# S5 inputs moved into the merge, moments made in the chain, down projection's first groups in passes

## The chip, the cores and the metric

The kernel runs on one core of a Trainium2 chip. The metric is the device time of one execution in microseconds (us), the median of several runs. TensorE (PE in the profile) multiplies matrices; VectorE (DVE), ScalarE (ACT), GpSimd (POOL) and SyncE (SP) do the rest and issue the DMAs. Each engine works through its own list of instructions in order, and an instruction that waits for another engine holds up all that stand behind it on its own.

## The reference, cut to what matters

One layer of a decoder with a hybrid token mixer, in float32, with T = 1024 tokens and 1024 channels:

```python
h = rms_norm(x, norm_mix_pre)
proj = h @ w_in          # RWKV columns | S5 input u | two gates
gates = jax.nn.sigmoid(proj[..., N_RWKV_COLS + S5_WIDTH:] + b_gate)
g_rwkv, g_s5 = jnp.split(gates, 2, axis=-1)
o_rwkv = rwkv7_branch(p_rwkv, ...) @ w_branch_rwkv
o_s5 = s5_branch(u_s5, ...) @ w_branch_s5
mixed = (g_rwkv * o_rwkv + g_s5 * o_s5) @ w_out
x = x + rms_norm(mixed, norm_mix_post)
h = rms_norm(x, norm_ffn_pre)
f = conv_ffn(h, w_up, conv_w, conv_b, w_down)    # 1024 -> 2 x 2816 -> 1024
x = x + rms_norm(f, norm_ffn_post)
```

In the RWKV branch a state S of 64 x 64 per head is carried over the tokens, and each head's outputs y are normalised over their 64 channels; these sums over a head are the moments of this text:

```python
S = S * w_t + sa * b_t + v_t * k_t ; y_t = S r_t
mean = jnp.mean(y, axis=-1, keepdims=True)
var = jnp.mean(jnp.square(y - mean), axis=-1, keepdims=True)
y = ((y - mean) * lax.rsqrt(var + LNX_EPS)) * lnx_w + lnx_b
```

The S5 branch ends in `y = gelu(y)` and `y * sigmoid(y @ w_glu + b_glu)`; the gelu of its scan's result is what this text calls an S5 input (of the gated unit).

## The kernel before, in words

Channels lie on the 128 partitions, time on the free axis, in two halves of 512 tokens. Each operand of a large product is split into a high part (a cast on ACT, lines 160 and 245) and a low part (a subtraction on DVE, lines 161 and 246), and each product is three matmuls of 128 x 128 by 128 x 512: high by high, high by low, low by high (lines 180, 181 and 182; in the down projection 1760, 1761 and 1762).

The stages, by the span's time: norm and input projection with the S5 scan (to 255 us); RWKV, gates and merge (to 760); output projection, norms and up projection (to 1290); down projection (to 1517); last norm.

RWKV is made in four units: two groups of four heads by two time halves, unit i having group i % 2 and half i // 2. Each unit runs through a front (operands `ar` and `bk`, masked products `gr` at lines 752 and 754, line 741 making the last part of `bk`), an inverse of small triangular matrices on DVE (lines 810 and 812, fed by the masked products through DMAs of POOL at lines 760 and 803), a level step (lines 835 to 841: transposes on DVE, products on PE, copies on ACT), a chain of eight chunks (lines 850 to 913) in which each chunk's state S (line 912) is read by the next chunk's matmuls (line 887), and an end, `rwkv_out`, which normalises the chunk outputs `yn` and transposes them (line 961).

The order of the instructions on PE is written out by hand: a planner interleaves the lanes of the units with a queue of fill work (gate tiles, gated sums, merged sums) by due times, the constants named T_. On the other engines a scheduler puts the instructions in order beforehand, by priority and dependence. So a step that one function issues can stand, on DVE, ACT or POOL, among those of quite other functions.

Half 0's branches are merged while units 2 and 3 run. `merge_values` makes the merge's operands; it is called among the gate tiles, which fall into the front of unit 3. It loads the four S5 inputs of half 0 (`s5_y`: a DMA of POOL at line 1233 and a gelu on ACT at 1234) and splits them (`s5_split`: a strided cast at 1241 and a subtraction at 1242). `merge` then makes eight gated sums (`gate`, with the product at line 1264), from the fourth on with one tile of the gated unit each (`glu_tile`), which reads the S5 inputs; and then eight merged sums (lines 1264, 1269 and the split at 251).

The down projection is seven products by Winograd's form of Strassen's scheme, each over eleven slices of the inner dimension in six groups, (0,1), (2,3), (10), (4,5), (6,7), (8,9). A product accumulates into four PSUM banks m; a step is the three matmuls of one slice and one bank. Its operands are made a group ahead into a ring of three sets, from weights and activations that DMAs bring into stage tiles; line 1715 makes the sums and differences of them, line 1712 takes the banks out.

## Time and profile before

| | |
|---|---|
| runs shown | 1533.64, 1539.38, 1544.39 us; median 1539.38 |
| profiled execution | 1531.82 us, span 1530.0 |
| PE busy | 1473.2 us (96%) |
| DVE busy | 1152.2 us (75%) |
| ACT busy | 724.5 us (47%) |
| POOL busy | 181.4 us (12%) |
| mean granted PE clock | 0.991 |

Times in the trace count from the span's start. In a group's row, `rp<-ar,bk` names the output and the inputs of an instruction; a wait is told as the engine, the tile and the line that waited, and what it waited for. The granted clock is the share of full speed at which PE was let run in that stretch. [...]

### The profile page before, as it was taken

The numbers are of one execution on the slowest core, as the hardware profiler recorded it, in microseconds if no ns is written. First come the engines' busy times: TensorE is split into PE (matmuls) and PEld (weight loads), VectorE is DVE, ScalarE is ACT, GpSimd is POOL, SyncE is SP. The second block draws the span as 40 slices with busy tenths as digits, with TensorE's granted clock in tenths as the row PEclk, the third lists the DMA queues.
The fourth block names the chain that finished last, engine by engine and source line by source line (L and its number), as shares of the span: only waits on it lengthen the run. The fifth ranks groups of instructions, "written<-read, shape, count | busy, mean of one in ns | idle before, by whom it ended". The sixth has DMA issues, their size and how long they took to land.

```text
span 1530.0 us, 23482 instructions
## 1 busy us (share of the span) xinstructions
PE 1473.2 (96%) x8622; PEld 1175.9 (77%) x8622; DVE 1152.2 (75%) x2115; ACT 724.5 (47%) x1201; POOL 181.4 (12%) x340
## 2 busy tenths in 40 slices
PE   7999999999999989989999999999999999999997
PEld 5788787787677666666778788888888888788885
DVE  8879974765555594874668779788888887698777
ACT  6455444331454552556525556455555555443452
POOL 0022111124121223020110011000000000000000
PEclk9999999999999999999999999999999999999999
DMA  6355344444333446442455575333333336953722
GB/s 215 114 157 164 104 138 144 142 135 142 110 119 109 123 138 173 147 156 71 141 183 183 179 251 186 104 114 109 114 117 110 111 117 207 337 173 124 238 79 110
DMA packets 121556, 225.23 MB, mean 147 GB/s; under 512 B 31024, under 2 KB 37168, under 8 KB 121440
## 3 DMA queue, kind: packets, MB, share of 16 engines
q1 hardware_dynamic: 90576, 154.77, 31.7%
q0 software_dynamic: 21024, 64.71, 12.6%
q10 hardware_dynamic: 9840, 4.24, 1.0%
q8 instruction: 68, 1.11, 0.3%
q14 instruction: 48, 0.39, 0.1%
HBM read 164.16 MB, written 57.41 MB: 145 GB/s over the span
## 4 chain that ended last, share of the span: by engine, by line
PE 70%; DVE 15%; DMA 5%; issue 5%; ACT 4%; POOL 0%; SPq 0%; DVEq 0%; ACTq 0%; POOLq 0%
PE gm L180 9%; PE gm L181 7%; PE gm L182 7%; PE rp L1583 5%; PE rp L1584 5%; PE rp L1585 5%; PE mm L1584 2%; PE mm L1583 2%; PE mm L1585 2%; DMA st<-in_w_down_dram 2%; PE ch L181 2%; PE ch L182 2%; PE mm L180 2%; PE ch L180 2%; PE mm L181 2%
## 5 line engine op out<-in xcount | busy, mean ns | idle before, releaser
L180 PE MATMUL gm<-hh,wh 128*128 128x512 f32 x688 | 289.6, 421 | 3.0 <-DVE ev L1046 1.9
L181 PE MATMUL gm<-hl,wh 128*128 128x512 f32 x688 | 271.1, 394 | 1.6 <-DVE hl L246 1.6
L182 PE MATMUL gm<-hh,wl 128*128 128x512 f32 x688 | 270.8, 394 | 0.0
L160 ACT CAST wh<-wf 128x512 fp32r<-128x512 f32 x181 | 111.5, 619 | 169.8 <-PE gm L181 92.9
L161 DVE TENSOR_TENSOR wl<-wf,wh 128x512 fp32r<-128x512 f32 x181 | 124.0, 689 | 78.1 <-ACT wh L160 77.2
L180 PEld LDWEIGHTS gm<-hh,wh 128*128 128x128 f32 x688 | 130.1, 189 | 36.3 <-DVE ev L1046 2.3
L182 PEld LDWEIGHTS gm<-hh,wl 128*128 128x128 f32 x688 | 130.0, 189 | 28.5
L181 PEld LDWEIGHTS gm<-hl,wh 128*128 128x128 f32 x688 | 130.4, 190 | 25.5 <-DVE hl L246 3.6
L1761 PE MATMUL d<-xl,wh 128*128 128x512 f32 x308 | 120.3, 390 | 3.1 <-DVE xl L246 3.0
L1760 PE MATMUL d<-xh,wh 128*128 128x512 f32 x308 | 120.1, 390 | 0.0
L1762 PE MATMUL d<-xh,wl 128*128 128x512 f32 x308 | 119.9, 389 | 0.0
L1583 PE MATMUL rp<-t,h 128*128 128x512 f32 x252 | 98.3, 390 | 1.4 <-ACT p L1597 1.4
L1585 PE MATMUL rp<-t,l 128*128 128x512 f32 x252 | 98.0, 389 | 0.0
L1584 PE MATMUL rp<-t,h 128*128 128x512 f32 x252 | 98.0, 389 | 0.0
L1761 PEld LDWEIGHTS d<-xl,wh 128*128 128x128 f32 x308 | 57.8, 188 | 16.6 <-DVE xl L246 4.7
L246 DVE TENSOR_TENSOR l<-r,h 128x1024 fp32r<-128x1024 f32 (+1 forms) x40 | 38.9, 972 | 38.2 <-ACT h L245 38.2
L245 ACT CAST h<-r 128x1024 fp32r<-128x1024 f32 (+1 forms) x40 | 34.0, 849 | 70.1 <-PE rp L1584 65.9
L1760 PEld LDWEIGHTS d<-xh,wh 128*128 128x128 f32 x308 | 57.8, 188 | 12.0
L1762 PEld LDWEIGHTS d<-xh,wl 128*128 128x128 f32 x308 | 57.8, 188 | 11.8
L1604 DVE SCALAR_TENSOR_TENSOR y<-zv,vecs,y 128x1023 f32<-128x1023 f32 (+1 forms) x42 | 53.8, 1281 | 10.2 <-ACT y L1602 10.2
L1583 PEld LDWEIGHTS rp<-t,h 128*128 128x128 f32 x252 | 47.2, 187 | 12.0 <-ACT p L1597 2.2
L1584 PEld LDWEIGHTS rp<-t,h 128*128 128x128 f32 x252 | 47.3, 188 | 9.7
(472 smaller groups left out, 3324.7 us busy)
## 6 DMA issues: line engine op xcount, KB each, us to landing
r<-in_w_up_dram SPq DMA_DIRECT2D x42, 512.0 KB, 3.5
wf<-in_w_in_dram SPq DMA_DIRECT2D x72, 256.0 KB, 3.1
st<-in_w_down_dram SPq DMA_DIRECT2D x55, 256.0 KB, 4.2
st<-ACT SPq DMA_DIRECT2D x44, 256.0 KB, 4.7
ACT<-y POOLq DMA_DIRECT2D x21, 512.0 KB, 2.9
GT<-ev POOLq DMA_DIRECT2D x32, 256.0 KB, 3.4
wf<-in_w_br_dram SPq DMA_DIRECT2D x32, 256.0 KB, 3.1
wf<-in_w_out_dram SPq DMA_DIRECT2D x32, 256.0 KB, 2.7
```

The lines of the kernel that those rows point to most:

```text
L160: self.last_wh = nc.scalar.copy(h[:, :n], f[:, :n])
L161: low = nc.vector.tensor_tensor(l[:, :n], f[:, :n], h[:, :n].bitcast(F32), ALU.subtract)
L180: mm(ps, a, xh[k], start=a0, stop=False)
L181: mm(ps, a, xl[k], start=False, stop=False)
L182: mm(ps, b, xh[k], start=False, stop=z0)
L1583: mm(ps, wh[:, c], xh, start=first and k == 0, stop=False, skip_group_check=True)
L1584: mm(ps, wh[:, c], xl, start=False, stop=False, skip_group_check=True)
L1585: mm(ps, wl[:, c], xh, start=False, stop=k == 3, skip_group_check=True)
L1604: V.scalar_tensor_tensor(y[:, lag:], z[:, 0:1024 - lag], self.vec(nme, i), y[:, lag:], ALU.mult, ALU.add)
L1760: mm(ps, wh[:, c], xh[:, x], start=start, stop=False, skip_group_check=True)
L1761: mm(ps, wh[:, c], xl[:, x], start=False, stop=False, skip_group_check=True)
L1762: mm(ps, wl[:, c], xh[:, x], start=False, stop=stop, skip_group_check=True)
```

## The change

Three parts, and constants.

1. **S5 inputs.** `merge_values` no longer loads, gelus and splits half 0's four S5 inputs. `merge` does it at gated sums 1 and 2, two at each (table `XS0`), in tiles of the pool `ev` with its three buffers. On POOL their loads now stand singly among the stores of unit 3's masked products (line 760): two stores, load 0, a gate tile's store, load 1, two stores, load 2, the store of line 765, load 3, four stores.
2. **Moments.** The chain makes a quarter's moments after chunks 1, 3, 5 and 7: a reduction of 256 elements a partition on DVE, a subtraction of the mean on DVE, a square on ACT, a reduction on DVE. `rwkv_out` keeps the scale of the variance, the reciprocal root and the multiplication, this now in two halves, one for each pair u of heads.
3. **Down projection.** A step's matmuls are ordered (wh, xh), (wl, xh), (wh, xl). The first group of each product goes over its steps in three passes, one for each of these pairs, over all four banks (span 4: products 1, 2 and 3) or two banks at a time (span 2: the other four).

`T_LN` is not used where it falls (`rwkv_out`'s first yield is thrown away for units 0 to 2); `T_LF` puts the last unit's transposes four steps of three matmuls earlier among their neighbours on PE. Otherwise the order on PE is the same up to the down projection.

```diff
...
         mm = nc.tensor.matmul
         S, pt, UV, gr, ar, bkn = self.S[d["g"]], d["pt"], d["UV"], d["gr"], d["ar"], d["bkn"]
         d["yn"] = self.tg("yn", 1, (128, 4, 2, 2, 64))
+        d["lm"], d["lv"] = [self.small.tile([128, 16], F32, tag=n, name=self.nm(n), bufs=2) for n in ("lm", "lv")]
         kw = dict(stop=True, skip_group_check=True)
         uh = [(u, h, HS[h], HS[1 - h]) for u in range(2) for h in range(2)]
         t0, t1 = HS
...
                 mm(psn[sl, u], bkn[:, u, c, sl], UV[:, (c + h) % 8, h, u], start=False, **kw)
             for u in range(2):
                 V.scalar_tensor_tensor(S[:, u], psn[:, u], pt[:, c, u:u + 1], spt[:, u], ALU.mult, ALU.add)
+            if c % 2:
+                self.moments(d, c // 2)
             yield 0.65, T_CH
+
+    def moments(self, d, j):
+
+        V = self.nc.vector
+        y = d["yn"][:, j].rearrange("p u h i -> p (u h) i")
+        mean, var = d["lm"][:, 4 * j:4 * j + 4], d["lv"][:, 4 * j:4 * j + 4]
+        sq = d["ar"][:, 0, 2 * j:2 * j + 2].rearrange("p c t -> p (c t)").rearrange("p (a i) -> p a i", i=64)
+        V.tensor_reduce(mean, y, AX.X, ALU.add)
+        V.scalar_tensor_tensor(y, mean.unsqueeze(2).to_broadcast([128, 4, 64]), -1.0 / 64, y, ALU.mult, ALU.add)
+        self.nc.scalar.activation(sq, y, AF.Square)
+        V.tensor_reduce(var, sq, AX.X, ALU.add)

     def urgent(self, gen):

...
             return r
         if final:
             ts = [factors(u) for u in range(2)]
-        yn = d["yn"].rearrange("p c u h i -> p (c u h) i")
-        mean = self.small.tile([128, 16], F32, tag="lm", name=self.nm("lm"), bufs=2)
-        V.tensor_reduce(mean, yn, AX.X, ALU.add)
-        V.tensor_scalar(mean, mean, 1.0 / 64, None, ALU.mult)
-        V.tensor_tensor(yn, yn, mean.unsqueeze(2).to_broadcast([128, 16, 64]), ALU.subtract)
-        var = self.small.tile([128, 16], F32, tag="lv", name=self.nm("lv"), bufs=2)
-        for j in range(2):
-            sq = free[:, j].rearrange("p (a i) -> p a i", i=64)
-            A.activation(sq, yn[:, 8 * j:8 * j + 8], AF.Square)
-            V.tensor_reduce(var[:, 8 * j:8 * j + 8], sq, AX.X, ALU.add)
+        var = d["lv"]
         V.tensor_scalar(var, var, 1.0 / 64, 64e-5, ALU.mult, ALU.add)
-        y = self.rsqrt(var, 16, "or")
-        V.tensor_tensor(yn, yn, y.unsqueeze(2).to_broadcast([128, 16, 64]), ALU.mult)
+        y = self.rsqrt(var, 16, "or").rearrange("p (c u h) -> p c u h", u=2, h=2)
+        for u in range(2):
+            yn = d["yn"][:, :, u]
+            V.tensor_tensor(yn, yn, y[:, :, u].unsqueeze(3).to_broadcast([128, 4, 2, 64]), ALU.mult)
         if not final:
             ts = [factors(u) for u in range(2)]
         yield 0, T_LF if final else T_LN
...

     def merge_values(self):

-        if not self.xs0:
-            for b in range(4):
-                y = self.hp[1].tile([128, 8, 64], F32, tag=f"hh{b}", name=self.nm("y"), bufs=1)
-                y = self.s5_y(y, b, 0)
-                self.xs0.append(self.pair(1, 4 + b))
-                self.s5_split(*self.xs0[b], y)
         if self.outs < 2:
             return
         for k in range(2):
...
         yield 0
         first = []
         for i in range(NK + MGAP):
+            for b in XS0.get(i, ()):
+                y = self.s5_y(self.ev(s8), b, 0)
+                xs.append(self.pair(1, 4 + b))
+                self.s5_split(*xs[b], y)
             if i < NK:
                 first.append(self.hp[0].tile([128, 512], F32, tag=f"h{'lh'[i // 4]}{i % 4}", name=self.nm("hl"), bufs=1))
                 yield from self.gate(0, i, 0, br[0:4], first[i], first[i])
...
         def p3(g):
             return operands(g, cS[g], cB[g])

-        def step(op, q, m, ps, start, stop):
+        def step(op, q, m, ps, start, stop, passes=(0, 1, 2)):
             (wh, wl), (xh, xl) = op
             c, x = slice(q * 512 + m * 128, q * 512 + m * 128 + 128), slice(q * 512, q * 512 + 512)
-            mm(ps, wh[:, c], xh[:, x], start=start, stop=False, skip_group_check=True)
-            mm(ps, wh[:, c], xl[:, x], start=False, stop=False, skip_group_check=True)
-            mm(ps, wl[:, c], xh[:, x], start=False, stop=stop, skip_group_check=True)
+            for k in passes:
+                w, y = ((wh, xh), (wl, xh), (wh, xl))[k]
+                mm(ps, w[:, c], y[:, x], start=start and k == 0, stop=stop and k == 2, skip_group_check=True)

         def bank(m):
             return self.ps.tile([128, 512], F32, tag=f"d{m}", name=self.nm("d"), bufs=1)

-        def product(prep, ps, first, evict, between=lambda g: None):
+        def product(prep, ps, first, evict, between=lambda g: None, span=2):

             for g in range(ng):
                 op = prep(g)
                 n = len(groups[g])
                 qm = [(q, m) for q in range(n) for m in range(4)]
-                if g in (0, ng - 1):
+                if g == ng - 1:
                     qm = [(q, m) for m in range(4) for q in range(n)]
+                if g == 0:
+                    for m0 in range(0, 4, span):
+                        for k in range(3):
+                            for m in range(m0, m0 + span):
+                                for q in range(n):
+                                    step(op, q, m, ps[m], first and q == 0, False, (k,))
+                    between(g)
+                    continue
                 for q, m in qm:
-                    step(op, q, m, ps[m], first and g == 0 and q == 0, g == ng - 1 and q == n - 1)
+                    step(op, q, m, ps[m], False, g == ng - 1 and q == n - 1)
                     if g == ng - 1 and q == n - 1:
                         evict(m)
                 between(g)
...
                 outputs(0, f[0], d["bc"], d["xs"])
                 d["xs1"] = resid(1)
         d, last = {}, []
-        product(p1, b, True, keep1)
-        product(p2, x, True, c11)
+        product(p1, b, True, keep1, span=4)
+        product(p2, x, True, c11, span=4)
         product(p5, x, True, lambda m: None)
         product(p6, b, False, keep2)
         product(p7, b, False, c22)
         product(p4, b, False, c21)
-        product(p3, x, False, c12, middle)
+        product(p3, x, False, c12, middle, span=4)
         ss, sums = bank(2), {}

         def resid_sum(m, b):
...
 T_US, T_TAB0, T_TAB, T_TRIG, T_SCAN = 5.0, 26.0, 20.0, 12.0, 13.0
 T_LD, T_LT = 14.0, 3.0
 NEVA = 4
-T_KN, T_BK, T_GR, T_INV, T_LV, T_CH, T_LN, T_LF = 12.0, 10.0, 2.5, 58.0, 1.0, 0.8, 16.0, 14.5
+T_KN, T_BK, T_GR, T_INV, T_LV, T_CH, T_LN, T_LF = 12.0, 10.0, 2.5, 58.0, 1.0, 0.8, 12.0, 12.0
 T_X, T_GLU = 3.0, 25.0
 T_N0, T_RS, T_N1, T_N2, T_N4, T_N5, T_N3 = 2.5, 4.0, 2.2, 5.0, 1.6, 24.0, 2.0
 NET = 5
 T_PN = 8.0
 KORD = (0, 4, 1, 5, 2, 6, 3, 7)
 MGAP = 3
+XS0 = {1: (0, 1), 2: (2, 3)}
 PACE, CREDIT = 0.8, 2.0
 NLD = 10
 NWH = 4
```

DVE at the front of unit 3. `bk` at L741 is what PE's L752 waits for; `hl<-y,hh` at L1242 are low parts of S5 inputs; `hl` and `wl` at L246 and L161 are low parts of the gate tiles' operands. Before, from just behind the first of four L1242:

```order
L812 TENSOR_TENSOR x_5303<-x_5303,tm_5399 128x16
L741 SCALAR_TENSOR_TENSOR bk_5750<-gr_5608,ld_5623 64x8x64
L1242 TENSOR_TENSOR hl_5951<-y_5947,hh_5950 128x512
L741 SCALAR_TENSOR_TENSOR bk_5750<-gr_5608,ld_5614 64x8x64
L1242 TENSOR_TENSOR hl_5958<-y_5954,hh_5957 128x512
L161 TENSOR_TENSOR wl_6074<-wf_6075,wh_6073 128x512
L1242 TENSOR_TENSOR hl_5965<-y_5961,hh_5964 128x512
L246 TENSOR_TENSOR hl_5969<-hl_5969,hh_5968 128x512
L246 TENSOR_TENSOR hl_5974<-hl_5974,hh_5973 128x512
L246 TENSOR_TENSOR hl_5979<-ld_5586,hh_5978 128x512
L161 TENSOR_TENSOR wl_6162<-wf_6163,wh_6161 128x512
L741 SCALAR_TENSOR_TENSOR bk_5750<-gr_5608,ld_5614 64x8x64
```

Now:

```order
L738 SCALAR_TENSOR_TENSOR ar_5769<-gr_5628 128x8x64 x2
L739 SCALAR_TENSOR_TENSOR gr_5628<-ld_5636,gr_5628 128x512
L739 SCALAR_TENSOR_TENSOR gr_5628<-ld_5645,gr_5628 128x512
L741 SCALAR_TENSOR_TENSOR bk_5770<-gr_5628,ld_5634 64x8x64
L161 TENSOR_TENSOR wl_6066<-wf_6067,wh_6065 128x512
L741 SCALAR_TENSOR_TENSOR bk_5770<-gr_5628,ld_5643 64x8x64
L741 SCALAR_TENSOR_TENSOR bk_5770<-gr_5628,ld_5634 64x8x64
L741 SCALAR_TENSOR_TENSOR bk_5770<-gr_5628,ld_5643 64x8x64
L161 TENSOR_TENSOR wl_6168<-wf_6169,wh_6167 128x512
L754 TENSOR_TENSOR gr_5628<-rp_6010,csts 128x4x128
L754 TENSOR_TENSOR gr_5628<-rp_6011,csts 128x4x128
```

The L1242 are gone from here (they stand behind the L754 and L764 of this unit), and the four L246 have moved ahead of the first L741.

DVE at the end of unit 2. `S` at L912 (now L913) is the last chunk's state; `yn` are the unit's outputs, `lm` and `lv` the sums for their mean and variance, `rsy` and `rsh` the steps of the reciprocal root; `ev` and `hl` with L1264, L1269 and L251 (now L1271, L1276 and L251) are merged sums. Before:

```order
L912 SCALAR_TENSOR_TENSOR S_2620<-chb_6911,pt_4549,spt_6917 128x64
L943 TENSOR_REDUCE lm_6990<-yn_6375 128x16
L161 TENSOR_TENSOR wl_7199<-wf_7200,wh_7198 128x512
L1264 SCALAR_TENSOR_TENSOR ev_6929<-hl_6928,gm_6937 128x512
L944 TENSOR_SCALAR lm_6990<-lm_6990 128x16
L912 SCALAR_TENSOR_TENSOR S_2620<-chb_6911,pt_4549,spt_6917 128x64
L1269 TENSOR_TENSOR ev_6929<-ev_6929,hl_6208 128x512
L945 TENSOR_TENSOR yn_6375<-yn_6375,lm_6990 128x1024
L251 SCALAR_TENSOR_TENSOR hl_6928<-ev_6929,hh_6927 128x512
L1264 SCALAR_TENSOR_TENSOR ev_6978<-hl_6977,gm_6986 128x512
L950 TENSOR_REDUCE lv_6994<-ar_4710 128x8
L161 TENSOR_TENSOR wl_7242<-wf_7243,wh_7241 128x512
```

Now:

```order
L913 SCALAR_TENSOR_TENSOR S_2620<-chb_6945,pt_4559,spt_6951 128x64 x2
L924 TENSOR_REDUCE lm_6396<-yn_6395 128x4
L1271 SCALAR_TENSOR_TENSOR ev_6963<-hl_6962,gm_6971 128x512
L161 TENSOR_TENSOR wl_7229<-wf_7230,wh_7228 128x512
L1276 TENSOR_TENSOR ev_6963<-ev_6963,hl_6228 128x512
L925 SCALAR_TENSOR_TENSOR yn_6395<-lm_6396,yn_6395 128x256
L251 SCALAR_TENSOR_TENSOR hl_6962<-ev_6963,hh_6961 128x512
L927 TENSOR_REDUCE lv_6397<-ar_4720 128x4
L956 TENSOR_SCALAR lv_6397<-lv_6397 128x16
L138 TENSOR_SCALAR rsy_7029<-lv_6397 128x16
L139 TENSOR_SCALAR rsy_7029<-rsy_7029 128x16
L141 TENSOR_TENSOR rsh_7030<-rsy_7029 128x16
```

The three steps over all of `yn` are gone; three of a quarter's four moments steps stand there, and the root begins eight rows behind S.

The end of the same stretch, where the outputs are multiplied (L953, now L960) and unit 3's level step takes its transposes (L835). Before, the transposes stood among the steps of the root:

```order
L251 SCALAR_TENSOR_TENSOR hl_6977<-ev_6978,hh_6976 128x512
L138 TENSOR_SCALAR rsy_7000<-lv_6994 128x16
L835 STREAM_TRANSPOSE ld_7182<-gr_5608 32x512
L139 TENSOR_SCALAR rsy_7000<-rsy_7000 128x16
L835 STREAM_TRANSPOSE ld_7182<-gr_5608 32x512
L161 TENSOR_TENSOR wl_7286<-wf_7287,wh_7285 128x512
```

Now:

```order
L143 SCALAR_TENSOR_TENSOR rsy_7029<-rsh_7030,rsy_7029 128x16
L960 TENSOR_TENSOR yn_6395<-yn_6395,rsy_7029 128x4x128 x2
L1271 SCALAR_TENSOR_TENSOR ev_7092<-hl_7091,gm_7100 128x512
L161 TENSOR_TENSOR wl_7316<-wf_7317,wh_7315 128x512
L1276 TENSOR_TENSOR ev_7092<-ev_7092,hl_6498 128x512
L970 SCALAR_TENSOR_TENSOR ar_4720<-rp_7158,vecs,ar_4720 128x512
L835 STREAM_TRANSPOSE ld_7212<-gr_5628 32x512
L251 SCALAR_TENSOR_TENSOR hl_7091<-ev_7092,hh_7090 128x512
L1271 SCALAR_TENSOR_TENSOR ev_7146<-hl_7145,gm_7154 128x512
L161 TENSOR_TENSOR wl_7322<-wf_7323,wh_7321 128x512
L1276 TENSOR_TENSOR ev_7146<-ev_7146,hl_6601 128x512
L835 STREAM_TRANSPOSE ld_7212<-gr_5628 32x512
```

Both L835 now stand behind the multiplication, the second one behind a merged sum's L1271, L161 and L1276.

ACT at the level step of unit 3. L841 copies what PE's L840 waits for; L1234 and L1241 (now L1241 and L1248) are gelus and casts of half 1's S5 inputs, `p` at L874 is a copy of the chain. Before:

```order
L839 COPY ld_7182<-chb_7181 32x256
L1241 CAST e_7151<-et_7148 128x512
L1234 ACTIVATE et_7155<-et_7155 128x512
L1234 ACTIVATE et_7162<-et_7162 128x512
L1234 ACTIVATE et_7763<-et_7763 128x512
L250 ACTIVATE hh_7238<-ev_7240 128x512
L841 COPY gr_5608<-chk_7179 32x8x32 x2
L1241 CAST e_7158<-et_7155 128x512
L1241 CAST e_7165<-et_7162 128x512
L160 CAST wh_7476<-wf_7478 128x512
```

Now:

```order
L841 COPY gr_5628<-chk_7209 32x8x32
L250 ACTIVATE hh_7268<-ev_7270 128x512
L841 COPY gr_5628<-chk_7209 32x8x32
L160 CAST wh_7508<-wf_7510 128x512
L841 COPY gr_5628<-chk_7209 32x8x32 x2
L1241 ACTIVATE et_7178<-et_7178 128x512
L1248 CAST e_7181<-et_7178 128x512
L1241 ACTIVATE et_7185<-et_7185 128x512
L874 COPY p_1383_7393<-chk_7388 128x128
L1248 CAST e_7188<-et_7185 128x512
```

All four L841 now stand ahead of the gelus.

## The prediction

> **What bounds the kernel now.** I read the page's head first, then the waits of TensorE (engine, tile and line <- what it waited for: us in total, times, longest), then the table of stretches (from:to, length, busy us of PE, PEld, DVE, ACT, POOL, granted TensorE clock, DMA share, GB/s).
>
> ```profile
> span 1530.0 us, 23482 instructions
> PE 1473.2 (96%) x8622; PEld 1175.9 (77%) x8622; DVE 1152.2 (75%) x2115; ACT 724.5 (47%) x1201; POOL 181.4 (12%) x340
> ```
>
> PE is busy for 1473.2 of 1530.0 us. The change issues the same matmuls on it, so all that can be gained is the 57 us in which PE stands still, and the stretches in which it runs at a lower clock. Nothing on DVE, ACT or POOL counts by itself; it counts where PE waits for it.
>
> ```profile
> PE rp L961 <- DVE yn L953: 5.6, 1, 5.6
> PE rp L752 <- DVE bk L741: 5.0, 1, 5.0
> PE chk L840 <- ACT gr L841: 2.1, 2, 1.7
> PE rp L736 <- ACT gr L734: 1.8, 1, 1.8
> PE chk L887 <- DVE S L912: 1.6, 2, 0.9
> ```
>
> The two longest single waits stand at places that the change touches: the front of RWKV unit 3 (L752 waits for L741) and the end of unit 2 (L961 waits for L953). The clock around them:
>
> ```profile
> 560.00:580.00 20.00, 15.05 (x69) 12.14 (x68) 15.72 (x29) 12.28 (x18) 9.90 (x17) 0.91 0.65 201
> 580.00:600.00 20.00, 19.77 (x222) 13.70 (x221) 10.52 (x16) 4.93 (x12) 7.81 (x14) 1.00 0.56 175
> 620.00:640.00 20.00, 18.27 (x184) 12.56 (x183) 18.92 (x63) 10.43 (x28) 1.07 (x2) 1.00 0.48 156
> 660.00:680.00 20.00, 14.05 (x78) 11.08 (x77) 15.27 (x32) 7.46 (x15) 2.98 (x6) 0.83 0.53 194
> 680.00:700.00 20.00, 17.95 (x200) 12.20 (x199) 11.92 (x17) 15.46 (x28) 1.07 (x2) 0.91 0.28 81
> 760.00:780.00 20.00, 19.02 (x86) 15.46 (x85) 14.50 (x33) 8.43 (x15) 1.07 (x2) 0.91 0.56 183
> 671.70:676.80 5.10, 5.10 (x16) 4.37 (x17) 2.92 (x4) 0.00 (x0) 0.00 (x0) 0.50 0.16 62
> ```
>
> A clock of 0.91 over 20 us is 0.09 x 20 = 1.8 us of full-speed work lost. Behind the wait of 5.6 PE was busy throughout 671.70 to 676.80 at 0.50, which lost 0.5 x 5.1 = 2.5.
>
> **The change part by part.** The sum is made against the profiled execution, 1531.8 us (span 1530.0); the median of the runs shown, 1539.4, is 7.6 higher, and I carry the difference over to it.
>
> *A, front of unit 3.* Timeline rows: start, length, engine, line, in brackets the idle time before and its releaser; the second row groups the line's four.
>
> ```profile
> 565.15 1.10 DVE L1242 TENSOR_TENSOR hl<-y,hh 128x512 fp32r<-128x512 f32 x1 [1.23 <-ACT hh L1241]
> L1242 DVE TENSOR_TENSOR hl<-y,hh 128x512 fp32r<-128x512 f32 x4 | 4.3, 1074 | 1.5 <-ACT hh L1241 1.5
> 566.26 0.67 DVE L741 SCALAR_TENSOR_TENSOR bk<-gr,ld 64x512 f32<-64x512 f32 x1
> 570.42 1.04 DVE L1242 TENSOR_TENSOR hl<-y,hh 128x512 fp32r<-128x512 f32 x1
> 573.90 0.69 DVE L741 SCALAR_TENSOR_TENSOR bk<-gr,ld 64x512 f32<-64x512 f32 x1
> 574.74 2.01 PE L752 MATMUL rp<-ar,bk 64*128 64x128 f32 x14 [4.95 <-DVE bk L741]
> ```
>
> PE waits for the third L741. The four L1242 ahead of it cost DVE 4.3 and 1.5 of waiting for ACT, together 5.8 against the wait of 4.95. The change takes them away from there. The four L246 stay ahead, and two L161 become one. So that L741 comes 5.8 earlier or more and the wait goes; what is late next is L736's wait (1.8), whose ACT work loses a gelu's company but not its own inputs, so I take none of it. The clock's 1.8 goes with the wait. Ends: -8.5 (4.95 + 1.8 + 1.8) and -2.5 (half of the wait stays); I take 4.95 + 1.8 = -6.8.
>
> *B, the S5 inputs' new place.* The four loads on POOL, eight gelu steps and casts on ACT and four L1242 now lie, by the order, among L754 and L760 of unit 3.
>
> ```profile
> 593.55 2.33 POOL L760 DMA_DIRECT2D md<-gr  x4 [6.18 <-DVE gr L754]
> 615.74 0.22 DVE L810 TENSOR_TENSOR tm<-x,mt 128x62 f32<-128x62 f32 x1
> ```
>
> DVE is busy there for 10.5 of 20 and ACT for 4.9, so the 5.8 have room. But a load of an S5 input that waits on POOL for its buffer now holds the L760 behind it, and through them the masked tiles that unit 3's inverse (L810, from 615.74) reads. Its cover is the 20 us from the end of the last L760 (595.9) to 615.7; without it the POOL wait passes through. Ends 0 and +3 (half of the POOL wait of 6.18); I take +1.5.
>
> *C, moments in the chain of unit 2.*
>
> ```profile
> 629.35 0.28 DVE L890 TENSOR_TENSOR p<-p,chk 128x128 f32<-128x128 f32 x1
> 654.37 0.28 DVE L912 SCALAR_TENSOR_TENSOR S<-chb,pt,spt 128x64 f32<-128x64 f32 x1 [0.42 <-PE chb L910]
> 654.60 1.22 DVE L943 TENSOR_REDUCE lm<-yn 128x16 f32<-128x1024 f32 x1
> 657.80 1.22 DVE L945 TENSOR_TENSOR yn<-yn,lm 128x1024 f32<-128x1024 f32 x1
> 662.50 0.68 DVE L950 TENSOR_REDUCE lv<-ar 128x8 f32<-128x512 f32 x1
> ```
>
> Before: 1.22 + 1.22 + 2 x 0.68 + one small step of 0.17 = 4.0. After: twelve steps of 256 elements a partition. Such a step lies between 0.28 (128 elements) and 0.68 (512); the straight line from 512 (0.68) to 1024 (1.22) gives 0.41, my value: 12 x 0.41 = 4.9, or 0.9 more per unit. Nine of the twelve, 3.7 us, come before the last chunk, where DVE is busy for 18.92 of 20 and PE has waited for S (L912), if only for 1.6 in all. Ends 0 (hidden) and +4.2 (12 x 0.68 - 4.0, all of it passed on); more work in that queue can't bring S forward, which excludes a gain. I take +2.0. In units 0 and 1, whose ends PE didn't wait for, I take nothing; their cover gone costs 0.9 each. [...]
>
> *D, end of unit 2.*
>
> ```profile
> 665.71 0.39 PE L182 MATMUL gm<-hh,wl 128*128 128x512 f32 x1
> 670.31 1.22 DVE L953 TENSOR_TENSOR yn<-yn,rsy 128x1024 f32<-128x1024 f32 x1
> 671.68 0.66 PE L961 MATMUL rp<-csts,yn 128*128 128x128 f32 x2 [5.58 <-DVE yn L953]
> ```
>
> From the last chunk's S (first half, 654.65) to the end of L953 (671.53) are 16.9 us; PE was free for the transposes at 671.68 - 5.58 = 666.10, so 11.5 are allowed. What now stands on DVE between the last S and the second half of the product: three moments steps of 0.41, eight 512-element steps of the merge at 0.68, two products of 0.68, twelve small ones at 0.17 = 1.2 + 5.4 + 1.4 + 2.0 = 10.0, and about 1 for waiting for PE and ACT in between: 11. That is just in time. I leave 1.0 of the wait standing: -5.58 + 1.0, and the clock's 2.5: -7.1. Ends: -8.1, and -2 (11 becomes 15). Both L835 of unit 3 now stand after the products, the second one behind three steps of a merged sum: 0 to 3 x 0.68 = +2.0, I take +1.0.
>
> *E, level of unit 3 and the last unit.*
>
> ```profile
> 687.10 1.67 ACT L1234 ACTIVATE et<-et 128x512 f32<-128x512 f32 x3
> 690.10 0.44 PE L840 MATMUL chk<-gr,ld 32*32 32x32 f32 x16 [1.69 <-ACT gr L841]
> 761.23 1.04 PE L961 MATMUL rp<-csts,yn 128*128 128x128 f32 x8
> 770.74 1.05 PE L264 MATMUL rp<-ones,sq 128*128 128x1 f32 x8 [0.98 <-DVE sq L1429]
> 360.27 1.16 PE L752 MATMUL rp<-ar,bk 64*128 64x128 f32 x14 [1.80 <-DVE ld L764]
> ```
>
> The L841 that PE waits for stands behind three gelus of 1.67 on ACT; these now come after all four L841: the wait of 1.69 goes, and 0.5 comes back where a chain copy now stands behind them. The last unit's transposes had no wait; they stand four steps of three matmuls earlier, which takes me to half of the next wait, 0.5. Both stretches show 1.8 of lost clock, but a wait of 1.80 at 360.27 was followed by no such loss, so the loss need not hang on the wait: I take half, 0.9 each. Together -1.2 - 0.9 - 0.5 - 0.9 = -3.5. Ends -6.3 (1.7 + 1.8 + 1.0 + 1.8) and +1. [...]
>
> *F, down projection.*
>
> ```profile
> 1302.55 0.50 PE L1761 MATMUL d<-xl,wh 128*128 128x512 f32 x1 [0.96 <-DVE xl L246]
> 1459.64 1.22 DVE L246 TENSOR_TENSOR wl<-st,wh 128x1024 fp32r<-128x1024 f32 x1
> 1460.78 1.22 DVE L246 TENSOR_TENSOR xl<-T,xh 128x1024 fp32r<-128x1024 f32 x1
> 1462.05 0.50 PE L1761 MATMUL d<-xl,wh 128*128 128x512 f32 x1 [1.09 <-DVE xl L246]
> 1505.96 0.50 PE L1761 MATMUL d<-xl,wh 128*128 128x512 f32 x1 [0.94 <-DVE xl L246]
> ```
>
> Those three waits are all that PE loses to operands here, and none is at a first group: the first is at product 1's second, the next at product 4's fourth, the last at product 3's last. The passes remove nothing. The step's new order asks for xl one matmul later, 0.2 saved at the first and third; at the middle one DVE now makes xl and then wl, and wl is asked for second: unchanged. -0.4. A first group in passes touches its accumulators sooner, against the evictions of the product before: ends -1.0 and +1.0.
>
> Sum: -6.8 + 1.5 + 2.0 - 7.1 + 1.0 - 3.5 - 0.4 = -13.3: 1518.5 on the profile, **1526** on the median. All good ends: -8.5 - 8.1 - 6.3 - 1.0 = -23.9, 1515; all bad: -2.5 + 3 + 4.2 - 2 + 2 + 1 + 1 = +6.7, 1546.
>
> **The rivals.** *The clock's loss moves instead of going.* The four places in the sum hold 1.8 + 2.5 + 0.9 + 0.9 = 6.1 of clock. A wait of 0.98 stands in a stretch at 0.91, one of 1.80 doesn't; with all waits at new times, others of the 50-odd us left may be hit. Then -13.3 + 6.1 = -7.2: 1532.
>
> *The moments hold the chain: slower.* The second reduce of a quarter waits for ACT's square on an engine that works in order, with the next S behind it. If each waits for one more ACT step of about 1.1 (two of the three gelus that take 1.67 at 687.10), sixteen quarters in four units give 17.6, and the longer steps 4 x 0.9 = 3.6: +21.2 in place of C, against -15.3 from the rest: +5.9, 1545. It decides from (15.3 - 3.6) / 16 = 0.73 per quarter on. For it: 18.92 of 20. Against: PE waited for S twice, 1.6 in all, so there was slack in nearly every chunk.
>
> *All covers hold*: the good ends of A, D and E without B and C: -18 to -24, about 1518.
>
> *The down projection's part does nothing*: 0.4 less, inside the forecast.
>
> **How the numbers follow.** Forecast (-8 to -18) 0.56, the moved clock 0.20, all covers 0.11, held chain 0.13. One per cent, about what this measurement can tell from no change, is 15.4 us: faster is below 1524.0. That takes all of the third case and somewhat under half of the first: 0.35. Slower needs about 1 us more per quarter than the tipping point (15.4 / 16): 0.05. The rest is 0.60. The range leaves out the best end and half of the held chain: 1514 to 1543.
>
> **What would show it.** A: no wait over 1 us at the L752 of unit 3, a full clock in 560 to 580. B: the first L810 of unit 3 not later against the matmuls around it. C: waits for S in unit 2's chunks of 1.6 or a little more; four of a microsecond would speak for the slower rival. D: the transposes of unit 2 with under 2 us of waiting, and no stretch at half clock behind. E: no wait for L841 behind gelus. F: waits in the down projection within 0.5 of 3.0 in all. The forecast is wrong if the two long waits shrink by less than 7 us, or if new waits above 5 us stand between 576 and 660.

## The result, and the profile after

The changed kernel takes 1525.25 us (median of 7 runs, 1521.61 to 1529.45), the kernel before 1539.38 beside it: ratio 0.9908, 95% interval 0.9886 to 0.9929, or 14.1 us less. A second set of runs gave 0.9889 (0.9860 to 0.9919). The forecast was 1526, 13.3 less; within 1% had the largest chance. The profiled execution has a span of 1519.7 us, 10.3 under that of before.

The page's head, and the longest waits of TensorE between 540 and 700 us of the changed kernel (L901, L888 and L874 are the chain's old L900, L887 and L873):

```profile
span 1519.7 us, 23525 instructions
PE 1473.9 (97%) x8622; PEld 1175.8 (77%) x8622; DVE 1152.9 (76%) x2147; ACT 727.5 (48%) x1209; POOL 181.0 (12%) x340
```

```profile
PE chk L840 <- ACT x L839: 2.6, 2, 2.2
PE chk L901 <- ACT p L874: 1.5, 1, 1.5
PE rp L792 <- ACT bkn L783: 1.3, 1, 1.3
PE chk L888 <- ACT p L874: 1.2, 2, 0.9
PE chb L838 <- DVE ld L835: 0.9, 1, 0.9
```

Both long waits, for L741 and for yn, are gone; DVE's busy time is the same (1152.9 against 1152.2). By the two heads PE stands still for 45.8 us (span less busy time) where it stood still for 56.8, and is busy 0.7 longer: the gain of this pair of executions is idle time. At the head of the list now stands ACT. The stretches, with the columns of the prediction:

```profile
560.00:580.00 20.00, 20.00 (x113) 15.89 (x111) 16.56 (x35) 6.65 (x11) 11.64 (x21) 1.00 0.74 206
580.00:600.00 20.00, 16.84 (x191) 11.19 (x190) 11.09 (x16) 10.95 (x17) 8.81 (x17) 0.88 0.60 198
600.00:620.00 20.00, 19.63 (x193) 13.98 (x193) 9.90 (x28) 9.59 (x26) 1.80 (x4) 0.95 0.49 125
620.00:640.00 20.00, 18.61 (x195) 13.05 (x194) 19.34 (x61) 12.00 (x32) 1.44 (x3) 1.00 0.53 159
660.00:680.00 20.00, 19.05 (x164) 14.66 (x164) 18.21 (x39) 11.29 (x24) 9.29 (x17) 1.00 0.72 228
680.00:700.00 20.00, 16.88 (x199) 11.73 (x194) 10.07 (x17) 14.21 (x29) 1.08 (x2) 1.00 0.27 81
760.00:780.00 20.00, 20.00 (x94) 16.67 (x93) 13.74 (x32) 7.01 (x13) 0.32 (x1) 1.00 0.61 186
```

560 to 580 is full and at full clock where before it was busy for 15.05 at 0.91; but 580 to 600, full before (19.77 at 1.00), is now busy for 16.84 at 0.88.

Since PE's order is the same up to the down projection, but for the last unit's eight transposes, each matmul can be looked up in both traces, and the difference of its start times tells where the time went (start before, start after; the last column is the prediction's term):

| up to | before | after | difference | change | predicted |
|---|---|---|---|---|---|
| L792 in front of unit 3 | 535.83 | 539.87 | +4.0 | +4.0 | none |
| matmul behind unit 3's first L752, its half clock all but over | 577.70 | 573.03 | -4.7 | -8.7 | A -6.8 |
| chunk of unit 2 (L910) | 619.37 | 621.75 | +2.4 | +7.1 | B +1.5 |
| chunk of unit 2 (L887) | 635.81 | 637.20 | +1.4 | -1.0 | C +2.0 |
| behind unit 2's transposes, their half clock all but over | 676.83 | 669.86 | -7.0 | -8.4 | D -7.1 |
| behind unit 3's L838 | 679.75 | 673.77 | -6.0 | +1.0 | L835 +1.0 |
| behind unit 3's L840 | 693.78 | 685.36 | -8.4 | -2.4 | E, level: -1.7 - 0.9 |
| end of unit 3's chain, ahead of the last unit's transposes | 758.28 | 752.88 | -5.4 | +3.0 | E, chain: +0.5 |
| behind the output projection's first sums | 775.57 | 767.66 | -7.9 | -2.5 | E, last unit: -0.5 - 0.9 |
| up projection | 867.82 | 858.43 | -9.4 | -1.5 | none |
| end of the span | 1530.0 | 1519.7 | -10.3 | -0.9 | F -0.4 |

D, the new wait for L835 and the level step came out within 1.3 us of their terms. B is almost five times its term, unit 3's chain lost 2.5 more than its own, and 4.0 us were lost ahead of everything that the prediction speaks of (5.1 more in half clock, 1.2 less in waits).

### The profile page after: what moved, and what is told of

Same layout as the page of the kernel before. It is cut to its first block, busy times and chain, and to the rows that moved or that the text cites. A ratio compares the mean times of both kernels' runs of the same rounds, so it can differ in the third digit from the quotient of the medians.

```text
span 1519.7 us, 23525 instructions
## 1 busy us (share of the span) xinstructions
PE 1473.9 (97%) x8622; PEld 1175.8 (77%) x8622; DVE 1152.9 (76%) x2147; ACT 727.5 (48%) x1209; POOL 181.0 (12%) x340
## 4 chain that ended last, share of the span: by engine, by line
PE 48%; DVE 3%; DMA 1%; ACT 1%; issue 1%; SPq 0%; DVEq 0%; ACTq 0%
PE d L1767 11%; PE rp L1588 5%; PE rp L1589 5%; PE rp L1590 5%; PE mm L1589 2%; PE mm L1588 2%; PE mm L1590 2%; PE ch L181 2%; PE ch L180 2%; PE mm L180 2%; PE ch L182 2%; PE mm L181 2%; PE mm L182 2%; PE gm L180 1%; PE gm L181 1%; PE gm L182 1%
## 5 line engine op out<-in xcount | busy, mean ns | idle before, releaser
L161 DVE TENSOR_TENSOR wl<-wf,wh 128x512 fp32r<-128x512 f32 x181 | 124.2, 690 | 77.1 <-ACT wh L160 75.5
L1767 PE MATMUL d<-xl,wh 128*128 128x512 f32 x308 | 112.8, 390 | 1.4 <-DVE xl L246 1.4
L1767 PE MATMUL d<-xh,wh 128*128 128x512 f32 x308 | 113.1, 391 | 0.7 <-DVE p L1717 0.7
L1767 PE MATMUL d<-xh,wl 128*128 128x512 f32 x308 | 112.8, 390 | 0.0
L246 DVE TENSOR_TENSOR l<-r,h 128x1024 fp32r<-128x1024 f32 (+1 forms) x40 | 38.9, 972 | 39.7 <-ACT h L245 39.7
L1588 PEld LDWEIGHTS rp<-t,h 128*128 128x128 f32 x252 | 47.3, 188 | 12.1 <-ACT p L1602 2.2
```

Source lines behind the costliest of these rows:

```text
L161: low = nc.vector.tensor_tensor(l[:, :n], f[:, :n], h[:, :n].bitcast(F32), ALU.subtract)
L246: self.split_ops = a, (eng or self.nc.vector).tensor_tensor(lo, x, hi.bitcast(F32), ALU.subtract)
L1588: mm(ps, wh[:, c], xh, start=first and k == 0, stop=False, skip_group_check=True)
L1767: mm(ps, w[:, c], y[:, x], start=start and k == 0, stop=stop and k == 2, skip_group_check=True)
```

## The experiments

Times are compared by their ratio to the kernel before in the same set of runs (its medians: 1538.7, 1541.2 and 1540.7 us in the three sets, so 0.001 is 1.5 us). The experiments' lines are named by each kernel's own numbers: those up to 857 are the same in all, the later ones a few lines apart.

Each timed run has its mean granted clock on record. What is missing to 1, times the span, is about the time lost to half clock (0.50 in the traces, as from 671.70 to 676.80 us before and from 596 to 600 in the changed kernel); it is called the clock part here, and its medians are given. It is 20.0 us for the kernel before in all three sets, and 15.2 and 13.7 for the changed kernel in its two sets. So of the 14 to 17 us won, about 5 to 6 are clock and the rest, near 10, is waiting. The clock is recorded to 0.001, which is 1.5 us.

**The S5 inputs, put back.**

```diff
 def merge_values(self):
+    if not self.xs0:
+        for b in range(4):
...
 def merge(self, mg):
-            for b in XS0.get(i, ()):
...
```

> The changed kernel, but with the S5 inputs of half 0 made in merge_values again, among the gate tiles. Theory 1 (from the two traces): their move takes away 8.7 us at the front of unit 3 (waits at L736 and L752 and the half clock behind), but gives back 7.0 between 580 and 603 us (L839's copies behind gelus on ACT, 2.8 us of waiting of PE, and a half clock behind it). Undone, the kernel takes 1525 + 2 = 1527 us, the wait at L752 of about 5 us and its half clock are there again and those at L840 near 592 us are gone. Rival, the sum of the prediction (-6.8 for the old place, +1.5 for the new): 1525 + 5 = 1530 us or more.

Measured: 1532.3 us, ratio 0.9948 (0.9926 to 0.9970), 6.2 us (0.0040) over the changed kernel's first ratio; the clock part is 19.1. The rival is nearer. A wait of 6 us did come, but not for L741 (see the kernel with the moments alone).

**The moments, put back.**

```diff
-            if c % 2:
-                self.moments(d, c // 2)
...
+        V.tensor_reduce(mean, yn, AX.X, ALU.add)
...
```

> The changed kernel, but with the moments made at the end of each unit again, over all of yn. Theory 1: the moments are worth 8.4 us at the end of unit 2 and 3 in the last unit, and cost nothing in the chain: 1525 + 10 = 1535 us, with a wait of 5 to 6 us of the transposes of unit 2 for yn. Rival, the moments take from the chain some of what they give at its end (prediction: +2.0, and up to 4.2): 1525 + 5 to 7 = 1531 us, and the stretch from 600 to 655 us is shorter by 2 us or more than in the changed kernel.

Measured: 1542.7 us, 1.0018 (0.9998 to 1.0038): 17 us over the changed kernel, and no faster than before although S5 inputs and down projection are the new ones. The clock part is 23.9, so about half of the 17 is clock. The waits of PE between 540 and 720 us of this kernel:

```profile
PE rp L961 <- DVE yn L953: 5.7, 1, 5.7
PE chb L838 <- DVE x L835: 5.2, 2, 4.7
PE chk L840 <- ACT gr L841: 2.6, 2, 1.7
PE chb L898 <- DVE p L890: 2.3, 1, 2.3
PE rp L736 <- ACT gr L734: 2.0, 1, 2.0
```

The wait for yn (term D) was expected. L736 and L838 for L835, 21 and 46 us behind unit 1's transposes (546.0), were not: the changed kernel waits at neither. Both theories had left unit 1 out. The rival's sign did not come: between the table's two chunk matmuls of unit 2 lie 19.4 us here, against 15.4 in the changed kernel.

**The moments alone, on the kernel before.**

```diff
+            if c % 2:
+                self.moments(d, c // 2)
...
-T_KN, T_BK, T_GR, T_INV, T_LV, T_CH, T_LN, T_LF = 12.0, 10.0, 2.5, 58.0, 1.0, 0.8, 16.0, 14.5
+T_KN, T_BK, T_GR, T_INV, T_LV, T_CH, T_LN, T_LF = 12.0, 10.0, 2.5, 58.0, 1.0, 0.8, 12.0, 12.0
```

> The kernel before, with the moments in the chain and the two constants alone. Theory 1 (the moments do most of it, at the end of unit 2 and, by a shorter end of unit 1, at the front of unit 3): 1538.7 - 6 to -9 = 1531 us. Rival (the two moves share the gain evenly, as the prediction's terms A and D have it, -6.8 and -7.1 with the moves' costs +1.5 and +2.0): 1538.7 - 5 = 1534 us, with the wait of 5 us at L752 of unit 3 for L741 as it was.

Measured: 1533.7 us, 0.9951 (0.9933 to 0.9970), 7.5 us less than before, while the changed kernel in the same set is 17 less by its ratio. Theory 1 is the nearer one. The waits for L734 at L736 and for L741 at L752 are gone although the S5 inputs stand in `merge_values` as before. At the next L752, which had no such wait, there is a new one. Timeline rows of PE, DVE and POOL of this kernel:

```profile
587.94 2.07 PE L752 MATMUL rp<-ar,bk 64*128 64x128 f32 x14 [6.41 <-DVE ld L764]
...
587.19 0.69 DVE L764 TENSOR_TENSOR ld<-rp,ld 128x512 f32<-128x512 f32 x1 [5.61 <-DMA ld<-RKV]
...
582.44 1.13 POOL L696 DMA_DIRECT2D ld<-RKV  x2
```

L764 on DVE waits for the values of unit 3, with PE's bank behind it; POOL issues their load (L696) only at 582.4, behind the S5 inputs' loads, the inverse's stores and four L760. In the changed kernel POOL issues them at 563.4 and 568.6:

```profile
563.37 0.54 POOL L696 DMA_DIRECT2D ld<-RKV  x1 [2.04 <-DVE tm L810]
568.58 0.60 POOL L696 DMA_DIRECT2D ld<-RKV  x1
```

The kernel with the S5 inputs put back shows the same: L696 at 586.8, and a wait of 6.0 for L764. So beside the new moments, what the S5 inputs' move is worth at unit 3's front are these 6 us in POOL's queue, not L1242's time on DVE. The S5 inputs' loads alone do not make it: in the kernel before, which has them at the same place, POOL issues both L696 at 561.4. It is the place of L696 in POOL's list that is another one.

**Unit 1's end as before, the others new.**

```diff
-            if c % 2:
+            if c % 2 and not (d["g"] == 1 and d["th"] == 0):
...
```

> The changed kernel, but unit 1 makes its moments over all of yn at its end, as before; units 0, 2 and 3 as in the changed kernel. Theory 1 (unit 1's end stood on DVE ahead of unit 3's front and unit 2's transposes): waits of 2 us at L736 and 4 to 5 us at L838 near 580 us come up, +6 to +10 us with a half clock behind the second: 1532 to 1535 us. Rival (the prediction, which took nothing for units 0 and 1, 0.9 at most): 1524 to 1526 us.

Measured: 1538.95 us, 0.9982 (0.9959 to 1.0005), 14 us over the changed kernel in its set, more than either theory gave. The chain of causes, first in the changed kernel, then in this one (DVE's last step of unit 2's inverse; POOL's loads behind it; PE):

```profile
563.68 0.19 DVE L812 TENSOR_TENSOR x<-x,tm 128x16 f32<-128x16 f32 x1
...
570.27 4.66 POOL L822 DMA_DIRECT2D gr<-xd  x8 [1.10 <-DMA xd<-x]
```

```profile
571.47 0.19 DVE L812 TENSOR_TENSOR x<-x,tm 128x16 f32<-128x16 f32 x1
...
580.14 4.65 POOL L822 DMA_DIRECT2D gr<-xd  x8 [2.10 <-DMA xd<-x]
...
589.61 0.31 PE L838 MATMUL chb<-x,gr 32*32 32x32 f32 x2 [3.83 <-DVE x L835]
```

Unit 1's end, unit 2's inverse and unit 3's front share DVE between 540 and 565 us, where it is busy for 18.0 to 18.5 of the 20 us from 540 to 560 in every kernel here. With the longer end the inverse ends 7.8 us later, but not by the end's length alone: its step of 108 elements is only 1.4 late (559.87 against 558.43), and the rest comes in the last dozen steps, most of which follow each other at once in the changed kernel and stand among steps of unit 3's front here. Its blocks make two trips through POOL's DMAs, and PE waits for the transposes. Behind it stands half clock (matmuls of 128 x 512 are 0.43 us apart from 593.5 to 598.2 us and 0.23 from 578 to 584), then later waits (2.2 at L899, 3.1 for yn). The 14 us hold all of these. The clock part is 23.1 in the timed runs, so about 9 of the 14 are clock; the profiled execution is the longest of the twelve (1549.6 us). Whether the old list with the longer end would have cost as much is not tested.

**Unit 2's end as before, the others new.**

```diff
-            if c % 2:
+            if c % 2 and not (d["g"] == 0 and d["th"] == 1):
...
```

> The changed kernel, but unit 2 makes its moments over all of yn at its end; units 0, 1 and 3 as in the changed kernel. Theory 2 (after the runs so far: unit 1's end is worth 14 us by way of unit 3's front, unit 2's end the 8.4 us that the two traces show there, and their losses overlap): 1525 + 6 to +9 = 1532 us, waits up to 583 us as in the changed kernel, a wait of 4 to 6 us of the transposes for yn near 672 us. Rival (term D's gain is bought by what unit 1 does, which brings the chain forward): 1525 + 2 or less.

Measured: 1535.5 us, 0.9971 (0.9949 to 0.9992), 10 to 13 us over the changed kernel (0.9971 against its 0.9908 and 0.9889), where theory 2 had 6 to 9. The wait for yn is 4.9, as term D has it; 2.3 at L899 and 1.7 at unit 3's L840 come with it, and the clock part is 23.0. Units 1 and 2 put back one by one cost 14 and 10 to 13, all four together 17: their losses overlap.

**Twice the reductions.**

```diff
         V.tensor_reduce(mean, y, AX.X, ALU.add)
+        V.tensor_reduce(mean, y, AX.X, ALU.add)
...
         V.tensor_reduce(var, sq, AX.X, ALU.add)
+        V.tensor_reduce(var, sq, AX.X, ALU.add)
```

> The changed kernel, with both reductions of each quarter's moments issued twice: 8 x 0.40 = 3.2 us more on DVE in each unit, 12.8 in all, with the same output. Theory 1 (the chain has room; only the last quarter of a unit counts): +0.8 at the ends of units 2 and 3, and little else: 1526 to 1528 us. Rival (the chain is bound by DVE, term C of the prediction): most of 12.8, 1533 us or more, and longer waits for S at L888 and for L891's output at L899.

Measured: 1537.3 us, 0.9975 (0.9951 to 0.9999): 13 us (0.0086) over the changed kernel. Theory 1 fell. But that 13 us come for 12.8 of DVE work is chance: the clock part is 22.3 (13.7 in the changed kernel), and by the heads of the two pages PE stands still 5.5 us longer (53.0 against 47.5 in the repetition below) and is busy 7.7 longer with the same matmuls. The waits between 540 and 720 us:

```profile
PE rp L970 <- DVE yn L962: 3.6, 2, 3.1
PE chb L838 <- DVE x L835: 3.6, 2, 2.5
PE chk L888 <- DVE S L913: 2.4, 1, 2.4
PE chb L899 <- DVE p L891: 2.2, 1, 2.2
```

DVE is the second bound from 540 to 670 us, in all three places at once: the inverse, the chain, the end. That term C measured -1.0 does not mean that the chain has room for 3.2 us more. The changed kernel came to it 7 us late from B, and DVE may have caught up in that time; no run separates this.

**The S5 inputs earlier, in tiles of their own.**

```diff
-XS0 = {1: (0, 1), 2: (2, 3)}
+XS0 = {0: (0, 1, 2, 3)}
...
-                y = self.s5_y(self.ev(s8), b, 0)
+                y = self.hp[0].tile([128, 8, 64], F32, tag=f"hh{4 + b}", name=self.nm("y"), bufs=1)
+                y = self.s5_y(y, b, 0)
```

> The changed kernel, with the four S5 inputs asked for at gated sum 0 and loaded into four tiles of their own instead of the three shared ev tiles, so that their loads on POOL wait for no buffer and the gelus stand ahead of all L839 copies. Theory 1: the loads come 4 to 10 us earlier, PE's waits for L839 (2.2 and 0.4) go, and with them the half clock of 596 to 602 us (about 3.5): 1525 - 3 to -6 = 1520 us. Rival, the wait only moves (the copies wait for the gelus all the same, or the masked stores behind the loads are late for the inverse): 1524 to 1527 us.

What this was to mend, in the changed kernel's timeline: ACT's gelus and casts (L1241, L1248), the copies behind them (L839) and PE that waits for these; and the stretch of four microseconds behind it:

```profile
586.51 1.20 ACT L1241 ACTIVATE ev<-ev 128x512 f32<-128x512 f32 x2
587.61 2.13 ACT L1248 CAST hh<-ev 128x512 fp32r<-128x512 f32 x2
...
592.30 1.02 ACT L839 COPY x<-chb 32x256 f32<-32x256 f32 x3
...
592.72 0.24 PE L840 MATMUL chk<-gr,x 32*32 32x32 f32 x2 [2.19 <-ACT x L839]
```

```profile
596.00:600.00 4.00, 4.00 (x39) 2.38 (x38) 1.99 (x4) 0.43 (x2) 2.23 (x5) 0.50 0.47 129
```

Measured: the waits at L840 and the half clock behind them are gone (590 to 610 us at 1.00 instead of 0.83), and the same matmul that starts at 620.23 in the changed kernel starts 6.1 us earlier in this one; at 586.04 the lead was 1.9, so 4.2 were won. But the time is 1528.0 us, 0.9927 (0.9897 to 0.9956), which can't be told from the changed kernel's 0.9908 (0.9886 to 0.9929): not faster. The gain was given back at unit 2's chain (L899), its end and unit 3's level step, as the waits between 540 and 720 us show:

```profile
PE rp L968 <- DVE yn L960: 3.9, 2, 3.1
PE chb L899 <- DVE p L891: 2.4, 2, 2.2
PE chk L840 <- ACT gr L841: 1.6, 1, 1.6
```

B's mechanism is shown by this; a saving it isn't, since DVE is late next, and half clock stands behind the new wait at L899 (matmuls of 128 x 512 are 0.43 us apart from 622.7 to 624 us and 0.23 from 626; the changed kernel has 1.00 from 612 to 680). Part of DVE's lateness is the order of its list: the second half of yn's product stands 3.7 us behind the first here (667.64 and 663.91), with the merge's steps between.

**The mean subtracted on GpSimd, for three quarters of each unit**, in the changed kernel and in the last one.

```diff
+        if j < 3:
+            P = self.nc.gpsimd
+            P.tensor_scalar(mean, mean, 1.0 / 64, None, ALU.mult)
+            P.tensor_tensor(y, y, mean.unsqueeze(2).to_broadcast([128, 4, 64]), ALU.subtract)
+        else:
...
```

> The changed kernel with the subtraction of the mean in the first three quarters of each unit on GpSimd, and nothing else. Theory 2 (in the changed kernel the waits of 2.8 us at L840 let DVE catch up, so that its chain has little left to gain): 1523 to 1525 us. Rival (DVE binds the changed kernel's chain too): 1525 - 4 = 1521 us or less.

> The changed kernel with the four S5 inputs at gated sum 0 in tiles of their own (as in hp0_0), and the subtraction of the mean in the first three quarters of each unit on GpSimd (a scale of four numbers and a subtraction) instead of DVE: 3 x 0.41 = 1.2 us less on DVE in each unit's chain. Theory 2 (what the earlier S5 inputs gained before 620 us, 6 us, was given back to DVE's backlog in unit 2's chain: waits of 2.2 at L899 and 3.9 for yn): these waits fall below 1 and 1.5, 1520 us. Rival (GpSimd's steps take longer than the time between two chunks, and the squares and DMAs behind them are late): 1528 us or more.

Measured: 1530.1 us, 0.9940 (0.9918 to 0.9962), and 1537.6 us, 0.9984 (0.9962 to 1.0006): slower than without by 5 to 8 and by 9 us. Theory 2 held in neither; the second rival's time came, but nothing shows its reason. Less work on DVE did not shorten its queue where it counts. Waits of the first of the two between 500 and 720 us:

```profile
PE chb L838 <- DVE x L835: 5.7, 2, 5.3
PE chk L888 <- DVE S L913: 2.7, 2, 1.4
PE chk L906 <- DVE UV L902: 1.4, 1, 1.4
```

DVE's and POOL's lists are set up in another way, and the steps left stand later: unit 2's last L812 stands at 568.9 (563.7 in the changed kernel), L822 at 578.8, and L838 waits for 5.3. Whether GpSimd's steps themselves (0.62 us for one of 256 elements) would have paid with the old lists is not settled by this.

**The down projection, undone and alone.**

```diff
-                for k in passes:
-                    w, y = ((wh, xh), (wl, xh), (wh, xl))[k]
...
+            mm(ps, wh[:, c], xh[:, x], start=start, stop=False, skip_group_check=True)
+            mm(ps, wh[:, c], xl[:, x], start=False, stop=False, skip_group_check=True)
+            mm(ps, wl[:, c], xh[:, x], start=False, stop=stop, skip_group_check=True)
```

> The changed kernel, but with the down projection's old order of matmuls. Theory 1 (the prediction's term F, 0.4 us): 1525.5 us, within what can be measured of the changed kernel; three waits of about a microsecond in the down projection. Rival, the passes hide something that the trace doesn't name: 1528 us or more. Up to the down projection its program is that of the changed kernel, so its trace is also a second look at that: theory 1 has the waits of PE at the same places within 0.1 us, and half-clock stretches that stand behind no wait of over 3 us at other places than in the first look.

> The kernel before, with the down projection's new order alone. Theory (term F, 0.4 us; the down projections seen so far take 214.2 to 215.3 us from first to last matmul with either order, 217 to 218 in some executions): 1538 us, within 2 us of the kernel before; the waits for xl at product 1's second and product 3's last group are 0.2 to 0.3 shorter. Rival: the passes are worth 3 us (the changed kernel without them stood 3 us above it in time).

Measured: undone, 1528.4 us, 0.9930 (0.9905 to 0.9955); alone, 1537.3 us, 0.9980 (0.9962 to 0.9998), 3.1 us under the kernel before. The waits between 1285 and 1520 us of the changed kernel without the new order, and of the kernel before with it:

```profile
PE d L1766 <- DVE xl L246: 5.3, 5, 1.5
```

```profile
PE d L1762 <- DVE xl L246: 1.4, 2, 0.7
PE d L1762 <- DVE p L1712: 0.5, 1, 0.5
```

The rival is nearer by the times; the traces put the part at 1.1 us against the kernel before (3.0 of waits to 1.4 + 0.5) and 3.4 against this second trace of the old order (5.3 to 1.9). The kernel with the moments alone is a third trace of the old order; its waits for xl are 4.4. Those in the products between the first and the last vary between executions with the old order (one of 1.1 before, three of 0.6 to 1.5 in the undone one, two of 0.8 and 1.7 with the moments alone). All eleven traces of the new order have two waits for xl, 0.7 and 0.6. At the first group of product 5 ten of the eleven have a new wait of 0.3 to 2.9, for the evictions of the product before. The clock is no part of it in the timed runs (15.3 undone, 20.7 alone).

**The changed kernel again.**

> The changed kernel as it is, as a control beside the next three, on their chip. Theory 1 (half-clock stretches that stand behind no long wait come and go from execution to execution): the same waits of PE as in the first look within 0.2 us, half-clock stretches at some of the places 255, 363, 463, 596 and 670 to 690 us and not at all of them, a time of 1525 us give or take 5. Rival (each stretch belongs to its place): the stretches of the first look again, 254, 463 and 596 us.

Measured: 1524.8 us, 0.9889. The stretch from 460 to 470 us in the kernel before, the changed kernel, the kernel with earlier S5 inputs (on PE and DVE the changed kernel's order up to 560 us) and this repetition:

```profile
460.00:470.00 10.00, 9.63 (x118) 7.18 (x117) 5.94 (x30) 4.20 (x10) 0.54 (x1) 1.00 0.11 40
```

```profile
460.00:470.00 10.00, 10.00 (x88) 7.42 (x90) 5.22 (x26) 1.78 (x4) 0.55 (x1) 0.66 0.07 28
```

```profile
460.00:470.00 10.00, 9.62 (x118) 7.15 (x117) 6.16 (x29) 4.17 (x10) 0.55 (x1) 1.00 0.11 35
```

```profile
460.00:470.00 10.00, 10.00 (x100) 7.79 (x100) 6.09 (x28) 2.15 (x5) 0.55 (x1) 0.83 0.20 74
```

The granted clock is 1.00 before, and 0.66, 1.00 and 0.83 for one and the same list of matmuls: theory 1 holds for this place. The stretch costs 3.4 us (0.34 x 10) in one execution and nothing in another. It is not a matter of chance alone, though: it stands at this place in six of the eight executions whose clock or matmuls were read there. With the old order of the down projection 460 to 470 us show 0.75, and matmuls of 128 x 512 follow each other at 0.43 us instead of 0.23 from 463, 466 and 468 us on in the two kernels with the mean on GpSimd and the one with the down projection alone. From 250 to 260 us the last three have 0.83, 1.00 and 1.00; behind the wait at L840 the changed kernel and its repetition both show 0.83 over 590 to 610 us. The repetition's waits are those of the first execution within 0.4 us, not 0.2 (2.5 and 2.2 at L840).

## Why the prediction was right, and where it wasn't

The time was right to 0.8 us, and the two waits that were to go did go. As an account of the parts it was right in half. (One slip: the best end, 1515, lies inside the range that is said to leave it out.)

*A.* Right in the place and nearly in size (-8.7 against -6.8; the 1.9 over it is mostly L736's wait of 1.8, which I had not dared to take). Wrong in the reason: the step "so that L741 comes 5.8 earlier" gave the gain to the four L1242. The kernel with the moments alone loses the same two waits with the S5 inputs where they were, and the kernel with the new S5 inputs but the old moments has no wait for L741 either. Each part alone is enough for that wait, and each alone opens another: 6.4 us for L764 by a load that POOL issues late, or 4.7 us for L835 by an inverse that DVE ends late.

*"In units 0 and 1, whose ends PE didn't wait for, I take nothing; their cover gone costs 0.9 each."* This is the step that failed worst. No wait names unit 1's end, but it stands on DVE ahead of unit 2's inverse and unit 3's front: put back by itself it cost 14 us. What the step had wrong is the path: it asked whether PE waits for this end, not what stands behind it on DVE. With this step mended, the moments are the main part of the change.

*B.* The term that was mis-sized: +1.5 taken, +7.1 measured, above its bound of +3. The bound looked at POOL and the L760 behind the loads. What was late was ACT: table load (1.28 us), gelus and casts ahead of L839, in a stretch whose 4.9 of 20 us I had called room. An average says nothing of the copies that have to pass in one microsecond. The path that the term was priced by cost nothing: unit 3's first L810 came 1.3 later (617.07 against 615.74) where PE's matmuls came 1.1 later. Of the 7.1, 3.8 are waits of PE, 2.6 of them at L840, and the rest is the half clock from 595 to 602 us.

*C.* +2.0 taken, -1.0 measured in this trace, but the doubled reductions show what the term was about: DVE has no slack for 3.2 us a unit. The rival of the held chain was not what happened, and its mechanism, a wait for the square in each quarter, did not show.

The steps themselves were sized well. The groups on DVE between 600 and 665 us:

```profile
L925 DVE SCALAR_TENSOR_TENSOR yn<-lm,yn 128x256 f32<-128x256 f32 x4 | 1.7, 418 | 0.0
L924 DVE TENSOR_REDUCE lm<-yn 128x4 f32<-128x256 f32 x4 | 1.7, 414 | 0.0
L927 DVE TENSOR_REDUCE lv<-ar 128x4 f32<-128x256 f32 x4 | 1.6, 408 | 0.0
```

0.41, as by the straight line.

*D.* Right: -8.4 against -7.1, and by its own working. From the last chunk's S (its first half, 656.29) to the end of the product are now 10.9 us, against the 11 worked out and 11.5 allowed:

```profile
656.01 0.48 DVE L913 SCALAR_TENSOR_TENSOR S<-chb,pt,spt 128x64 f32<-128x64 f32 x2 [0.43 <-PE chb L911]
...
665.88 1.29 DVE L960 TENSOR_TENSOR yn<-yn,rsy 128x512 f32<-128x512 f32 x2
...
667.15 1.03 PE L968 MATMUL rp<-csts,yn 128*128 128x128 f32 x8
```

The transposes start without a wait, and L835's new wait is 0.95 against 1.0.

*E.* Level step and last unit right or better (-2.4 and -2.5 against -2.6 and -1.4). What came back behind the gelus in unit 3's chain was 3.0 and not 0.5: the chain's copies (L874) stand among the gelus that had been put behind L841, and PE waits 1.5 and 0.9 for them.

*F.* Right that the first groups had nothing to lose, but mis-sized: the middle wait, which I called unchanged, is gone, and the part is worth 1 to 3 us and not 0.4.

*The rival of the moved clock* happened beside the forecast in this pair of executions: half clock begins at 254, 462 and 595 us in the changed kernel, and at 575, 670, 691, 773 and 865 in the kernel before (both also have 0.50 near 15 us and at the span's end). The 4.0 us lost ahead of 540 are this, at matmuls that the change doesn't touch. It is also why one profile's differences of 3 us are no evidence by themselves here. Over the timed runs it did not happen: the clock part fell by 5 to 6 us, near the 6.1 of clock that the sum had counted on. One list of matmuls shows 0.66, 1.00 and 0.83 at one place. The stretch from 462 us has no wait ahead of it (PE is busy for 11.88 of the 12 us before), so a long wait just ahead is not the only way to half clock.

So the right total came out of errors that cancelled, which is luck. Between the two profiled executions, A, C, D, the last unit, F and a half clock near 866 us that only the kernel before has gave 9.1 us more than taken (the level step's 0.2 less is in it); B, unit 3's chain and the stretch ahead of 540 us took 12.1 more. That makes -10.3 in place of -13.3 for this pair; over the timed runs it was -14.1. The pair is narrower because the profiled execution of the kernel before lost little clock: about 13 us by its mean of 0.991, against 20.0 in the timed runs; that of the changed kernel lost about 12, against 15.2.
